# The lo part of the keys on both partition halves: score matmuls of 128 rows

## The chip, the cores and the metric

The kernel runs on one core of a Trainium2 chip. The core has a tensor engine (PE) for matmuls, VectorE (DVE), ScalarE (ACT) and GpSimd (POOL) for everything elementwise, and SyncE (SP), whose queue here issues the loads of weights. Each engine works through its own list of instructions in order and waits on semaphores for the others. The metric is device time in microseconds of one execution; lower is better.

## The reference

One decoder layer on 256 tokens of width 1024, in float32: a SwiGLU half-step, then a mixer stage, a memory cross-attention and a second SwiGLU half-step, each followed by a layer norm. The mixer stage runs a state-space branch (SSD) beside a sparse attention (DSA); the change is in DSA.

```
q_idx, k_idx, w_idx: index queries (16 heads of 64), one index key of 64, 16 head weights
score[q, s] = sum over h of relu(q_idx[q, h] . k_idx[s]) * w_idx[q, h] / 4, causal
keep the 64 best keys s of every query q
s[q, h, k]  = q[q, h] . (w_uk c_kv)[k, h] / 8 - slope[h] * (q - k), on the kept keys
o[q, h]     = softmax(s) (w_uv c_kv)
```

c_kv is a normalised latent of 256 per token, from which keys and values of the 16 heads of 64 are made.

## The kernel before

Every float32 operand a is split on the chip into hi (a rounded to the float32r format) and lo = a - hi; a product is hi.hi + hi.lo + lo.hi, three passes on PE that accumulate in PSUM (`mm3`). `split` (line 144) makes hi with a cast on ACT and lo with a subtraction on DVE. Weights are loaded in pieces of 128 x 1024 into four `raw` buffers and split into `whi` and `wlo`, six buffers each (`weight`, line 89). A block of work on PE (`a_block`) is 24 matmuls of 128 x 256.

**The scores.** Heads are 64 wide, half of the 128 partitions. `project` (line 633) therefore packs the queries: in one tile hi stands on one partition half and lo on the other. The first score matmul contracts over all 128 rows, the packed queries against keys whose hi stands on both halves (`kh`), and so gives hi.hi + lo.hi in one pass. The second takes the 64 rows of the queries' hi against the 64 rows of the keys' lo:

```
self.mm(o, q[:, hh // 2, ts], kh, True, False)
self.mm(o, q[r, hh // 2, ts], kl[r], False, True)
```

`scores` (line 646) does this for two blocks of 128 queries: four matmuls per head into one of two score banks (`ps_s`). It runs for 16 heads of the index (line 664, keys `kidxh` and `kidxl`), whose relu on ACT frees the bank and whose sum over the heads is made on DVE into `acc`, and for 16 heads of the attention (`softmax_in`, line 687, keys of the tile `kv`). `kidxl` is made from a transposed key that already stands on both halves, so all its 128 rows are filled.

**Keys and values.** `keys_values` (line 748) runs four times, for four heads each. It makes the keys in a PSUM bank and copies them out: per pair of heads two ACT copies (hi to both halves) and one DVE subtraction (lo to one half), then the values' hi and lo of token block 0 (`vh`, `vl`), all in one tile `kv` of 2048 columns: 1024 for hi, 512 for lo, 512 for the values.

**The order.** `fly` (line 117) interleaves three streams, DSA, SSD and a filler (keys and values, the gates, the SSD output projection), by an estimate of PE time: a stream yields how long it wants to wait for the other engines. After the index heads come 16 rounds of maximum and replacement on DVE (the top-k) while PE does filler work; then step by step (line 734) scores of one head, the transposes of the head two steps earlier and the values of the head three steps earlier, with 2.4 us (by the estimate) of filler between. The SSD stream ends with a product by silu(z) on DVE (line 608), a mean of squares on ACT, a power on POOL and a scaling on ACT (line 616); PE then transposes the result. On each engine the framework that builds the program settles the final sequence by its own schedule, so a change of one instruction can shift neighbours.

Of the kernel before, what the change touches and what calls it, by code (L numbers as in the profile page):

```python
"""Hybrid decoder layer (macaron SwiGLU, Mamba-2 SSD beside DSA attention, memory
cross-attention, SwiGLU; DeepNorm post-LayerNorms) on one core.

float32 products go through the tensor engine as three float32r passes: every
operand a is split on the chip into hi (a rounded to float32r) and lo = a - hi,
and a.b = hi.hi + hi.lo + lo.hi accumulates in PSUM.  Small products stay float32.
"""
# [12 lines left out]
F32 = mybir.dt.float32  # L20
F32R = mybir.dt.float32r
# [4 lines left out]
P = 128  # L26
T = 256
# [6 lines left out]
HD = 64  # L34
# [4 lines left out]
ALPHA = 2.0 ** 0.25  # L39
# [11 lines left out]
class Layer:  # L51
# [37 lines left out]
    def weight(self, ap, piece=1024, pool=False):  # L89
        """loads, split into (hi, lo) in pieces of columns; pool: GpSimd makes the last lo."""  # L90
        out = []
        for c in range(0, ap.shape[1], piece):
            raw = self.raw()[:, :piece]
            hi = self.wp.tile([P, 1024], F32R, tag="whi", name=self.nm("whi"), bufs=6)[:, :piece]
            lo = self.wp.tile([P, 1024], F32R, tag="wlo", name=self.nm("wlo"), bufs=6)[:, :piece]
            self.nc.sync.dma_start(raw, ap[:, c:c + piece])
            self.split(raw, hi, lo, self.nc.gpsimd if pool and c else self.nc.vector)
            out.append((hi, lo))
        return out
# [17 lines left out]
    def fly(self, *streams):  # L117
        """emits several streams of work in one order: a stream yields after a piece either
        how long (us of matmul work) its next piece should wait for the other engines, or the
        name of a result that another stream marks as done."""  # L120
        live = [[g, self.pe, None] for g in streams]
        while live:
            ok = [e for e in live if e[2] is None or e[2] in self.done]
            now = [e for e in ok if e[1] <= self.pe]
            e = now[0] if now else min(ok, key=lambda e: e[1])
            self.pe = max(self.pe, e[1])
            e[2] = None
            try:
                r = next(e[0])
            except StopIteration:  # L130
                live.remove(e)
                continue
            if isinstance(r, str):
                e[2] = r
            else:
                e[1] = self.pe + r

    def mm3(self, out, a, b, start, stop):
        """out (+)= a^T b; a, b = (hi, lo)."""
# [8 lines left out]
    def a_block(self, ps, w, xT):  # L148
        """w: (hi, lo) [p, 128] per K block, stationary; ps [128 features, 256 tokens]."""
# [3 lines left out]
    def a_unit(self, ap, xT):  # L153
        """two 128-column blocks, [p, (2, kb, 128)], by 256 tokens in one bank."""
# [11 lines left out]
    def b_part(self, ps, w, xT, tb, k, start, stop):  # L166
        """tokens of block tb stationary, one K block w (hi, lo) [p, n] moving."""
# [11 lines left out]
    def b_chunk(self, wap, xT, evac, width=512):  # L179
        """[2, p, (4 kb, width)] columns, both token blocks in turn."""  # L180
# [32 lines left out]
    def constants(self):  # L213
# [7 lines left out]
        # attention keys: [0:256] for the queries of block 1, [256:384] for block 0  # L221
# [27 lines left out]
    def ln_params(self, i):  # L249
        """(scale, shift) of layer norm i, each as two halves of the columns."""  # L250
        out = []
# [13 lines left out]
    def layer_norm(self, r, st, gb, dst):  # L265
        """r [128, 1024] with bn statistics st; dst may be r."""
# [11 lines left out]
    def res_evac(self, ps, c, r, x, scale, st):  # L278
        """r = scale * ps + x in the columns from c, with their statistics."""
# [11 lines left out]
    def ffn_in(self, win, xT, slots, first=None, by_token=0):  # L291
        """silu(gate) * up as hi/lo by features; the first by_token units run one token block
        after the other, so that the matmuls need not wait for the second."""
# [35 lines left out]
    def first_units(self, xT):  # L329
        """tokens and the first two units of FFN 1 K block by K block, as they arrive; the  # L330
        tensor engine and the activation tables are warmed up meanwhile."""
# [32 lines left out]
    def ffn_out(self, wout, act, finish, skew=3, last=False):  # L364
        """last: the columns that end last are finished in two parts."""
# [27 lines left out]
    def z_proj(self, xT):  # L393
        """silu(z), token-major; block 0 of the tokens runs ahead."""
# [12 lines left out]
    def xbc(self, xT, xtok, bc):  # L407
        """convolution and silu by features; x goes back to token-major."""
# [30 lines left out]
    def small_proj(self, xT):  # L439
        """c_kv, dt, w_idx and k_idx, token-major."""  # L440
# [17 lines left out]
    def latent(self, cT):  # L458
        """normalised c^T as hi/lo."""
# [18 lines left out]
    def k_index(self, kidx):  # L478
        """k_idx^T on both halves of the partitions."""
# [7 lines left out]
    def softplus(self, x, n):  # L487
        """log(1 + exp(x)) = max(x, 0) + 2 atanh(e / (2 + e)), e = exp(-|x|), x [128, n]."""
# [19 lines left out]
    def ssd_decay(self):  # L508
        """dt, the cumulated decays, and these as rows on every partition (DMA)."""
# [30 lines left out]
    def ssd(self, zs, xtok, bc, yT):  # L540
        """y takes the place of x in xtok."""
# [85 lines left out]
    def dsa(self, xT, kidx, cT, oT):  # L627
        """index scores, top-k, attention over the selected keys; o^T as hi/lo."""
# [4 lines left out]
        def project(name, u, scale):  # L633
            """(hi; lo) of the even heads and (lo; hi) of the odd ones on the partition halves."""
# [11 lines left out]
        def scores(q, hh, kh, kl):  # L646
            """kh: hi on both partition halves, kl: lo."""
            r, q = slice((hh % 2) * HD, (hh % 2 + 1) * HD), q[hh % 2]
            ps = self.psum("s")
            for tb in range(NTB):  # L650
                o, ts = ps[:, (1 - tb) * 256:(2 - tb) * 256], slice(tb * P, (tb + 1) * P)
                self.mm(o, q[:, hh // 2, ts], kh, True, False)
                self.mm(o, q[r, hh // 2, ts], kl[r], False, True)
# [25 lines left out]
        # attention  # L679
# [7 lines left out]
        def softmax_in(h):  # L687
            u, hh = h // 4, h % 4
            kv = self.kv[u]
            ps = scores(qs[u], hh, kv[0][:, hh % 2, hh // 2, :], kv[1][:, hh // 2, :])  # L690
# [11 lines left out]
        def turn(h):  # L702
            """p^T: key block 0 by all queries as hi/lo, key block 1 by the queries of block 1."""
# [10 lines left out]
        def values(h):  # L714
# [6 lines left out]
            # both heads of a pair are stationary, one of them is meant  # L721
# [26 lines left out]
    def keys_values(self, u, cT):  # L748
        """keys of four heads by features (hi of the even heads and of the odd ones on both
        partition halves, lo), their values by tokens (hi/lo of block 0; block 1)."""  # L750
# [4 lines left out]
        kl = s[:, 1024:1536].rearrange("p (a b) -> p a b", b=T)  # L755
        vh, vl = s[:, 1536:1792], s[:, 1792:]
# [5 lines left out]
        for i in range(2):  # L762
            a, b = slice(i * HD, (i + 1) * HD), slice((1 - i) * HD, (2 - i) * HD)
            nc.scalar.copy(kh[a, i], ps[a])
            nc.vector.tensor_sub(kl[a], ps[a], kh[a, i].bitcast(F32))
            nc.scalar.copy(kh[b, i], ps[a])
        yield 0.0
# [85 lines left out]
    def proj_ln(self, wap, inT, x, gb, done, hooks=()):  # L853
        """x <- LN(x + in W) in place, x pre-scaled by ALPHA; the last K blocks of the input
        come late, and token block 0 ends before block 1."""
# [33 lines left out]
    def run(self):  # L889
        nc, t = self.nc, self.t  # L890
# [96 lines left out]
def layout(x, mem, ffn1_w_in, ffn1_w_out, ln1_g, ln1_b, w_in, conv_w, conv_b, dt_bias, a_log, d_skip,  # L987
# [5 lines left out]
    def feats(w):                       # [1024, 256 n] -> [n, p, (2, kb, 128)]  # L993
# [3 lines left out]
    def toks(w, width=512):             # [1024, width n] -> [n, 2, p, (4 kb, width)]  # L997
# [3 lines left out]
    def ffn(win, wout, by_token=0):  # L1001
# [4 lines left out]
        if not by_token:                # the first two units by K block: [k, (gate, up) x 2, 128]  # L1006
# [43 lines left out]
```

## Time and profile before

| | us |
|---|---|
| median of 3 runs | 835.6 |
| lowest and highest | 834.26, 835.91 |
| span of the profiled execution | 833.3 |
| PE, DVE, ACT, POOL busy in it | 816.3, 560.8, 424.1, 68.1 |
| index heads on PE | about 297 to 347 |
| attention heads on PE | about 367 to 480 |

The span runs from the first to the last instruction of the profiled execution; its own time is the span and what lies around it, which the profile does not show. A row of a timeline has the start, the length and the instruction, out<-in with the program's names, and in brackets the idle time before it and what ended it. Matmuls are pipelined: one is listed with 0.28 us and the next starts after 0.12 us, so costs on PE are read from start to start, and PE's busy time is no measure of work done. The form 64*128 or 128*128 is the height and width of the stationary operand. A row of busy times has the length of the stretch, the busy time of each engine with its number of instructions, the clock that PE was granted (1.00 is 2.4 GHz, 0.50 is 1.2 GHz), and the share and rate of the DMA engines.

### The profile page before, as it was taken

Reading aid. Unit: us, or ns where it says so; the run is one execution under the profiler, and the core shown is the slowest. Engines: PE = TensorE matmul, PEld = TensorE weight load, DVE = VectorE, ACT = ScalarE, POOL = GpSimd, SP = SyncE. Lnnn points to the kernel's source line nnn. Section 1 sums busy time; section 2 is a strip of 40 time slices with the busy share of each in tenths; the row PEclk is TensorE's granted clock in tenths of the full one; section 3 lists DMA queues with packets and bytes.
Section 4 is the critical chain, followed back from the end, with each engine's and each line's share of the span. In section 5 each row is a group of like instructions: output and inputs, shape, how many; then the busy total and the mean of one; then the engine's idle time right before and its main releaser. Section 6 shows DMA issues by size and latency. Waiting matters only on the chain.

```text
span 833.3 us, 14320 instructions
## 1 busy us (share of the span) xinstructions
PE 816.3 (98%) x5726; PEld 758.1 (91%) x5726; DVE 560.8 (67%) x870; ACT 424.1 (51%) x700; POOL 68.1 (8%) x69
## 2 busy tenths in 40 slices
PE   8999999999989899999999999999999999999996
PEld 7999999887889887899999998889988999999885
DVE  5665555449598988598778767965659755555445
ACT  5564444324666584477566545454444644444430
POOL 1100000000024351130000000100001000000000
PEclk9999999999999998999999999999999999999998
DMA  7886555554556513226444355685434755555531
GB/s 246 275 281 212 178 181 184 194 176 130 193 191 240 180 49 107 72 77 217 150 126 153 117 174 182 199 271 172 151 119 134 260 184 179 187 190 179 185 120 51
DMA packets 39923, 142.97 MB, mean 172 GB/s; under 512 B 4592, under 2 KB 4896, under 8 KB 39472
## 3 DMA queue, kind: packets, MB, share of 16 engines
q1 hardware_dynamic: 38016, 134.63, 49.0%
q0 software_dynamic: 1840, 7.43, 2.9%
q8 instruction: 45, 0.74, 0.4%
q14 instruction: 22, 0.18, 0.1%
HBM read 140.97 MB, written 1.06 MB: 170 GB/s over the span
## 4 chain that ended last, share of the span: by engine, by line
PE 89%; DVE 4%; issue 4%; DMA 1%; ACT 1%; POOL 0%; SPq 0%; DVEq 0%; ACTq 0%; POOLq 0%
PE ps_mm L111 79%; PE ps_s L111 5%; DVE wlo L146 2%; PE ps_t L115 2%; PE ps_t L111 2%; DMA raw<-in_ffn_in_dram 1%; DVE wa L430 1%; ACT whi L145 0%; DVE spp L503 0%; DVE bcT L430 0%; POOL rstd L262 0%; DVE bst L285 0%; ACT L432 0%; SPq L349 0%; DVE x L282 0%
## 5 line engine op out<-in xcount | busy, mean ns | idle before, releaser
L146 DVE TENSOR_TENSOR wlo<-raw,whi 128x1024 fp32r<-128x1024 f32 (+2 forms) x245 | 302.2, 1236 | 184.8 <-ACT whi L145 183.3
L145 ACT CAST whi<-raw 128x1024 fp32r<-128x1024 f32 (+2 forms) x253 | 262.4, 1041 | 222.1 <-PE ps_mm L111 111.5
L111 PE MATMUL ps_mm<-x1Th,whi 128*128 128x256 f32 x384 | 112.4, 293 | 0.0
L111 PE MATMUL ps_mm<-x1Tl,whi 128*128 128x256 f32 x384 | 110.9, 289 | 0.0
L111 PE MATMUL ps_mm<-x1Th,wlo 128*128 128x256 f32 x384 | 110.8, 289 | 0.0
L111 PE MATMUL ps_mm<-x0Th,whi 128*128 128x256 f32 x352 | 99.7, 285 | 1.4 <-ACT whi L145 1.3
L111 PE MATMUL ps_mm<-x0Tl,whi 128*128 128x256 f32 x352 | 99.2, 283 | 0.0
L111 PE MATMUL ps_mm<-x0Th,wlo 128*128 128x256 f32 x352 | 98.3, 284 | 0.7 <-DVE wlo L146 0.7
L111 PE MATMUL ps_mm<-x3Th,whi 128*128 128x256 f32 x304 | 86.2, 284 | 0.0
L111 PE MATMUL ps_mm<-x3Th,wlo 128*128 128x256 f32 x304 | 86.0, 283 | 0.0
L111 PE MATMUL ps_mm<-x3Tl,whi 128*128 128x256 f32 x304 | 86.0, 283 | 0.0
L111 PEld LDWEIGHTS ps_mm<-x1Th,whi 128*128 128x128 f32 x384 | 75.5, 197 | 1.3
L111 PEld LDWEIGHTS ps_mm<-x1Tl,whi 128*128 128x128 f32 x384 | 75.5, 197 | 0.4 <-issue 0.4
L111 PEld LDWEIGHTS ps_mm<-x1Th,wlo 128*128 128x128 f32 x384 | 75.7, 197 | 0.1
L111 PEld LDWEIGHTS ps_mm<-x0Th,whi 128*128 128x128 f32 x352 | 67.7, 192 | 2.5 <-ACT whi L145 2.5
L111 PEld LDWEIGHTS ps_mm<-x0Th,wlo 128*128 128x128 f32 x352 | 66.9, 192 | 1.3 <-DVE wlo L146 1.3
L111 PEld LDWEIGHTS ps_mm<-x0Tl,whi 128*128 128x128 f32 x352 | 67.7, 192 | 0.0
L111 PE MATMUL ps_mm<-whi,ah 128*128 128x512 f32 x154 | 60.4, 392 | 0.0
L111 PE MATMUL ps_mm<-wlo,ah 128*128 128x512 f32 x154 | 60.1, 390 | 0.0
L111 PE MATMUL ps_mm<-whi,al 128*128 128x512 f32 x154 | 59.9, 389 | 0.0
L111 PEld LDWEIGHTS ps_mm<-x3Tl,whi 128*128 128x128 f32 x304 | 58.4, 192 | 0.0
L111 PEld LDWEIGHTS ps_mm<-x3Th,wlo 128*128 128x128 f32 x304 | 58.4, 192 | 0.0
(305 smaller groups left out, 1708.9 us busy)
## 6 DMA issues: line engine op xcount, KB each, us to landing
raw<-in_ffn_in_dram SPq DMA_DIRECT2D x87, 512.0 KB, 4.4
raw<-in_ffn_out_dram SPq DMA_DIRECT2D x44, 512.0 KB, 4.4
raw<-in_w_xbc_dram SPq DMA_DIRECT2D x16, 512.0 KB, 4.3
raw<-in_w_gate_dram SPq DMA_DIRECT2D x16, 512.0 KB, 3.6
raw<-in_w_z_dram SPq DMA_DIRECT2D x8, 512.0 KB, 4.4
raw<-in_w_qidx_dram SPq DMA_DIRECT2D x8, 512.0 KB, 4.1
raw<-in_w_q_dram SPq DMA_DIRECT2D x8, 512.0 KB, 3.7
raw<-in_w_pssd_dram SPq DMA_DIRECT2D x8, 512.0 KB, 4.1
```

The lines of the kernel that those rows point to most:

```text
L111: self.nc.tensor.matmul(out, a, b, start=start, stop=stop)
L115: self.nc.tensor.transpose(out, in_, self.ident)
L145: self.nc.scalar.copy(hi, src)
L146: (engine or self.nc.vector).tensor_sub(lo, src, hi.bitcast(F32))
L430: self.last_conv = nc.vector.scalar_tensor_tensor(v[:, d:], src[:, :T - d], cw[:, 3 - d:4 - d], v[:, d:], op0=ALU.mult, op1=ALU.add)
```

## The change

The lo of the keys now stands on both partition halves, as hi does. The second score matmul then takes the whole packed queries (128 rows) against it; it adds lo.lo to the product. For this `keys_values` makes two DVE subtractions per pair of heads instead of one, after both ACT copies, and `kl` takes 1024 columns of the tile `kv`. The values' hi and lo move to a buffer of the tag `w2c` (two buffers, also used by the SSD stream and the cross-attention). The index keys need nothing new. Comments and docstrings are gone from the file as well, with no effect on the program.

```
         def scores(q, hh, kh, kl):
-            r, q = slice((hh % 2) * HD, (hh % 2 + 1) * HD), q[hh % 2]
+            q = q[hh % 2]
...
                 self.mm(o, q[:, hh // 2, ts], kh, True, False)
-                self.mm(o, q[r, hh // 2, ts], kl[r], False, True)
+                self.mm(o, q[:, hh // 2, ts], kl, False, True)
...
-            ps = scores(qs[u], hh, kv[0][:, hh % 2, hh // 2, :], kv[1][:, hh // 2, :])
+            ps = scores(qs[u], hh, kv[0][:, hh % 2, hh // 2, :], kv[1][:, hh % 2, hh // 2, :])
...
-        kl = s[:, 1024:1536].rearrange("p (a b) -> p a b", b=T)
-        vh, vl = s[:, 1536:1792], s[:, 1792:]
+        kl = s[:, 1024:].rearrange("p (i a b) -> p i a b", i=2, b=T)
+        v0 = self.small([P, 2, T], "w2c", F32R, 2)
+        vh, vl = v0[:, 0, :], v0[:, 1, :]
...
             nc.scalar.copy(kh[a, i], ps[a])
-            nc.vector.tensor_sub(kl[a], ps[a], kh[a, i].bitcast(F32))
             nc.scalar.copy(kh[b, i], ps[a])
+            nc.vector.tensor_sub(kl[a, i], ps[a], kh[a, i].bitcast(F32))
+            nc.vector.tensor_sub(kl[b, i], ps[a], kh[a, i].bitcast(F32))
```

The sequence of PE keeps its matmuls, since the estimate counts columns and these are the same. What moves is seen on ACT and DVE. First ACT at the first unit of keys, in the midst of the index heads: `kv` are the copies of the keys and the cast of the values, `wa<-ps_s` the relus, `whi` casts of weights, `w2a` the scaling of the next index queries. Before:

```order
L666 ACTIVATE wa_3255<-ps_s_3250 128x384
L145 CAST whi_3661<-raw_3660 128x1024
L766 CAST kv_3204<-ps_mm_3206 64x512
L764 CAST kv_3204<-ps_mm_3206 64x512
L145 CAST whi_3774<-raw_3773 128x1024
L766 CAST kv_3204<-ps_mm_3206 64x512
L641 ACTIVATE w2a_3328<-ps_mm_3267 64x512
L666 ACTIVATE wa_3339<-ps_s_3334 128x384
L666 ACTIVATE wa_3352<-ps_s_3347 128x384
```

And now:

```order
L666 ACTIVATE wa_3258<-ps_s_3253 128x384
L145 CAST whi_3658<-raw_3657 128x1024
L145 CAST whi_3664<-raw_3663 128x1024
L765 CAST kv_3204<-ps_mm_3207 64x512
L766 CAST kv_3204<-ps_mm_3207 64x512
L145 CAST whi_3777<-raw_3776 128x1024
L641 ACTIVATE w2a_3331<-ps_mm_3270 64x512
L666 ACTIVATE wa_3342<-ps_s_3337 128x384
L666 ACTIVATE wa_3355<-ps_s_3350 128x384
```

Before, the second copy of the first pair of heads (766) stands here, then the two of the second pair (764, 766) with a weight cast between. Now the first pair's second copy stands ahead of this piece, right behind its first, and only the second pair's two copies (765, 766) are left, one behind the other. The cast, the scaling and the relus behind them keep their places.

Then DVE at the same place: `kv` are the subtractions of the keys (and, at 128 x 256, of the values), `acc` the sum over the index heads, `w2b` and `E` the SSD stream, `wlo` the lo of a weight. Before:

```order
L580 TENSOR_TENSOR E_2639<-E_2639,w2b_3182 128x1024
L765 TENSOR_TENSOR kv_3204<-ps_mm_3206,kv_3204 64x512
L669 SCALAR_TENSOR_TENSOR acc_3015<-wa_3230,widx_2227,acc_3015 128x256
L669 SCALAR_TENSOR_TENSOR acc_3015<-wa_3230,widx_2227,acc_3015 128x128
L146 TENSOR_TENSOR kv_3204<-ps_mm_3234,kv_3204 128x256
L669 SCALAR_TENSOR_TENSOR acc_3015<-wa_3255,widx_2227,acc_3015 128x256
L669 SCALAR_TENSOR_TENSOR acc_3015<-wa_3255,widx_2227,acc_3015 128x128
L765 TENSOR_TENSOR kv_3204<-ps_mm_3206,kv_3204 64x512
L571 TENSOR_TENSOR w2b_3264<-ps_t_3259,triu 128x512
L146 TENSOR_TENSOR wlo_3383<-raw_3381,whi_3382 128x1024
L580 TENSOR_TENSOR E_2643<-E_2643,w2b_3264 128x1024 x2
L642 SCALAR_TENSOR_TENSOR w2a_3328<-ps_mm_3267,w2a_3328 64x512
```

And now:

```order
L580 TENSOR_TENSOR E_2639<-E_2639,w2b_3182 128x1024
L767 TENSOR_TENSOR kv_3204<-ps_mm_3207,kv_3204 64x512
L768 TENSOR_TENSOR kv_3204<-ps_mm_3207,kv_3204 64x512
L669 SCALAR_TENSOR_TENSOR acc_3015<-wa_3233,widx_2227,acc_3015 128x256
L669 SCALAR_TENSOR_TENSOR acc_3015<-wa_3233,widx_2227,acc_3015 128x128
L146 TENSOR_TENSOR w2c_3205<-ps_mm_3237,w2c_3205 128x256
L669 SCALAR_TENSOR_TENSOR acc_3015<-wa_3258,widx_2227,acc_3015 128x256
L669 SCALAR_TENSOR_TENSOR acc_3015<-wa_3258,widx_2227,acc_3015 128x128
L767 TENSOR_TENSOR kv_3204<-ps_mm_3207,kv_3204 64x512
L768 TENSOR_TENSOR kv_3204<-ps_mm_3207,kv_3204 64x512
L571 TENSOR_TENSOR w2b_3267<-ps_t_3262,triu 128x512
L146 TENSOR_TENSOR wlo_3386<-raw_3384,whi_3385 128x1024
```

Each subtraction of the keys has a second one behind it, and the values' lo goes to `w2c`; all that follows stands two rows later.

## Rows read from the trace of the kernel before

**Rows 1.** The page, sections 1 and 4: engines, and shares of the chain.

```profile
PE 816.3 (98%) x5726; PEld 758.1 (91%) x5726; DVE 560.8 (67%) x870; ACT 424.1 (51%) x700; POOL 68.1 (8%) x69
...
PE 89%; DVE 4%; issue 4%; DMA 1%; ACT 1%; POOL 0%; SPq 0%; DVEq 0%; ACTq 0%; POOLq 0%
```

**Rows 2.** Busy time by stretch; then PEclk, DMA share, GB/s.

```profile
299.46:313.20 13.74, 13.74 (x99) 12.19 (x98) 13.52 (x18) 10.31 (x16) 6.19 (x4) 1.00 0.00 0
316.40:323.10 6.70, 6.70 (x24) 5.36 (x24) 4.44 (x9) 2.62 (x4) 1.34 (x1) 0.50 0.10 35
299.46:339.70 40.24, 40.24 (x240) 33.56 (x238) 34.69 (x48) 20.71 (x33) 11.15 (x6) 0.92 0.29 92
354.50:366.90 12.40, 12.40 (x106) 12.40 (x105) 12.31 (x58) 8.86 (x18) 3.40 (x2) 1.00 0.25 86
382.25:411.01 28.76, 28.76 (x218) 26.71 (x216) 22.25 (x44) 19.81 (x45) 0.64 (x1) 1.00 0.55 173
411.01:439.77 28.76, 28.76 (x218) 26.72 (x216) 22.55 (x46) 18.20 (x45) 0.54 (x1) 1.00 0.44 139
```

**Rows 3.** Timeline of PE (start, length), first attention head.

```profile
366.78 0.28 PE L111 MATMUL ps_mm<-x1Th,wlo 128*128 128x256 f32 x1
366.90 1.21 PE L111 MATMUL ps_s<-kv,w2a 128*128 128x256 f32 x4
368.04 0.39 PE L111 MATMUL ps_mm<-x1Th,whi 128*128 128x256 f32 x1
368.27 0.28 PE L111 MATMUL ps_mm<-x1Tl,whi 128*128 128x256 f32 x1
```

**Rows 4.** Timeline of PE, first scores of the cross-attention.

```profile
571.64 0.28 PE L111 MATMUL ps_s<-mkh,w2a 128*128 128x256 f32 x1
571.76 0.27 PE L111 MATMUL ps_s<-mkl,w2a 128*128 128x256 f32 x1
```

**Rows 5.** Instructions on the score banks: the full-height weight load.

```profile
L111 PEld LDWEIGHTS ps_s<-mkl,w2a x16: 187/188/190, 571.6 to 614.2; 128*128 128x128 f32 x16
```

**Rows 6.** Timeline of PE while the clock is at its lower level.

```profile
317.30 0.58 PE L111 MATMUL ps_s<-kidxh,w2e 128*128 128x256 f32 x1
317.81 0.58 PE L111 MATMUL ps_s<-kidxl,w2e 64*128 64x256 f32 x1
...
319.72 0.41 PE L111 MATMUL ps_mm<-x1Th,wlo 128*128 128x256 f32 x1
319.93 0.41 PE L111 MATMUL ps_mm<-x1Th,whi 128*128 128x256 f32 x1
```

**Rows 7.** Instructions on the kv tile: the subtraction (min/median/max ns).

```profile
L765 DVE TENSOR_TENSOR kv<-ps_mm,kv x8: 678/689/695, 309.4 to 449.4; 64x512 fp32r<-64x512 f32 x8
```

**Rows 8.** Timeline of ScalarE, first unit of keys.

```profile
310.12 0.58 ACT L766 CAST kv<-ps_mm 64x512 fp32r<-64x512 f32 x1 [1.95 <-DVE kv L765]
...
314.53 0.49 ACT L666 ACTIVATE wa<-ps_s 128x384 f32<-128x384 f32 x1 [0.52 <-PE ps_s L111]
```

**Rows 9.** Timeline of all engines: from silu(z) to the SSD transposes.

```profile
339.70 1.22 DVE L608 TENSOR_TENSOR xtok<-xtok,zs 128x1024 f32<-128x1024 f32 x1
...
341.03 0.42 ACT L612 ACTIVATE wa<-xtok 128x256 f32<-128x256 f32 x1 [5.17 <-DVE xtok L608]
...
347.02 1.42 POOL L262 TENSOR_TENSOR rstd<-rstd,mhalf 128x4 f32<-128x4 f32 x1 [10.32 <-DVE rstd L261]
...
348.47 1.71 ACT L616 ACTIVATE xtok<-xtok,rstd 128x256 f32<-128x256 f32 x4 [0.47 <-POOL rstd L262]
...
354.52 1.03 PE L115 MATMUL ps_t<-ident,xtok 128*128 128x128 f32 x8
```

**Rows 10.** Timeline of PE, the first head's transposes.

```profile
381.76 0.49 PE L115 MATMUL ps_t<-ident,wa 128*128 128x128 f32 x3
```

**Rows 11.** Timeline of PE after an idle time.

```profile
245.16 0.47 PE L115 MATMUL ps_t<-ident,wb 128*128 128x128 f32 x1 [2.89 <-DVE cTl L475]
...
245.65 0.41 PE L111 MATMUL ps_mm<-x1Th,whi 128*128 128x256 f32 x1
```

## The prediction

> **What bounds the kernel now.** I read the page's busy totals and its chain first: the tensor engine (PE) is busy 98% of the span, and 89% of the chain that ended last is PE [rows 1]. A total hides stages, so next the busy time by stretch [rows 2]. Where the changed matmuls lie, from 297 to 473 us, PE is busy for the whole of every stretch, and the view of waits has no wait of PE at all from 300 to 500 us. So PE sets the pace there, and each microsecond that leaves its stream counts, until some other engine cannot follow. VectorE (DVE) is the one to watch: 34.69 of 40.24 us in the index stage, 12.31 of 12.40 where the top-k begins, 78% (22.25 of 28.76) over four heads of attention [rows 2]. Third, the order of PE's instructions in time, for what a score matmul costs.
>
> **Part 1, the score matmuls.** A head is a group of four: hi, lo for one token block, hi, lo for the other. The hi ones contract over 128 rows, the lo ones over 64. Ordinary 128-row matmuls of this shape start 0.12 us apart (366.78 to 366.90). The group starts at 366.90, the matmul behind it at 368.04, and the next at 368.27: five starts take 1.37 us where five ordinary ones take 0.60 [rows 3]. The excess is 0.77 us, and it is paid at each change of height: the matmul behind the group still pays one (0.23 to the next start), though it is itself ordinary. Cross-attention has the control: its scores, hi and lo both over 128 rows, of the same shape, start 0.12 us apart [rows 4]. After the change the group has that form throughout, so I take the whole 0.77 us out. There are 16 groups of the index and 16 of the attention: 16 x 0.77 = 12.3 us each, 24.6 in all, on PE, which waits for nothing.
>
> A rule of the Trainium skill speaks against this ("TensorE: Matmul & The Clock Gate", Part 3, The mechanism): a weight load overlaps a running matmul only where the row groups differ. By it a full-height load behind a full-height matmul is exposed, and the change would give nothing. The trace disagrees: full-height loads of 188 ns run under matmuls that start 0.12 us apart [rows 4, 5].
>
> **Part 2, the clock.** In two places the granted clock falls from the upper level (2.4 GHz) to the lower (1.2 GHz): from 316.35 to 323.1 and from 347.1 to 350.5. In the first the granted clock reads 0.50 [rows 2]. Both times PE had just run score groups nearly back to back, in which a start came each 0.31 us. At the lower level score matmuls start 0.51 apart instead of 0.31, and ordinary ones 0.21 instead of 0.12 [rows 6]. Over both places that is 16 + 10 ordinary ones at 0.093, 2.4 us, and some nine starts of score matmuls at up to 0.20, 1.8 us: 4.2 us. When score groups run as densely as the rest, what went before the falls is gone; I let these 4.2 us go too. Ends: 0 (the falls come all the same) and 4.2.
>
> **Part 3, the evacuation of the keys.** Each of four units gets two more DVE subtractions of 64 x 512 from PSUM. The same form is there: 0.69 us each [rows 7], so 8 x 0.69 = 5.5 us of DVE, 1.4 per unit; reading one partition half and writing the other is what the split of the queries (line 642) does already, so I see no surcharge. ScalarE's two copies of a pair of heads now stand together, as the order shows: its wait of 1.95 us for the first subtraction [rows 8] moves to the first copy of the unit's second pair, which waits for the first pair's subtractions, now two: some 0.6 us later. Queued behind it are a weight cast, the scaling of the next queries and the relus that free the two score buffers. The values' move into a buffer of their own costs nothing: the same cast and subtraction write it, and no transfer is added; the weights come in the same sequence, but for one exchange of neighbours.
>
> **Part 4, what is late next: the index stage.** On PE alone, the transposes of the SSD output that stand at 354.52 [rows 9] would come 12.3 + 4.2 = 16.5 us earlier, at 338.0. Their input hangs on DVE: a product by silu(z) that starts at 339.70, then four squares on ScalarE, the power on GpSimd (1.42) and the scaling [rows 9]. DVE was idle 40.24 - 34.69 = 5.55 us between 299.46 and 339.70 [rows 2]; if it never idled, with 1.4 us of new subtractions, that product would start at 335.5. From there to the first scaled half (half of 1.71) it was 9.6 us, with relus that waited for PE between; the pure work is 1.22 + 4 x 0.42 + 1.42 + 0.86 = 5.2 us. So the input is there between 340.7 and 345.1. I take 8 us (the chain shares both queues with other work), 343.5. PE is then held 5.5 us, and the stage gives 16.5 - 5.5 = 11.0 us. An earlier hold lies inside this one: the third group of the second index unit needs a score buffer that a relu of ScalarE frees; that relu ran at 314.53 behind the key copies [rows 8], and PE would want the buffer near 311.
>
> The top-k comes next on DVE, but PE needs its result late, for the first head's transposes at 381.76 [rows 10], 15 us behind the stretch in which DVE does the top-k [rows 2]. This gap absorbs the rest of DVE's lag.
>
> **Part 5, the attention.** 16 groups give 12.3 us. Over four heads PE would need 28.76 - 4 x 0.77 = 25.7 us, DVE 22.25 + 1.38 = 23.6 (then 22.55 + 1.38 = 23.9): 92 to 93% [rows 2]. What PE loses to that, no stretch of the attention shows. Lower end 0: with DVE at 99% (354.50 to 366.90) and at 98% (299.46 to 313.20) PE lost nothing [rows 2], because weights are split several blocks ahead. Upper end 7 us, a share as in the index stage (5.5 of 12.3 and more). I take 1.5, since 92% is below both stretches without loss.
>
> **Part 6, idle and clock.** Before 245.16 PE idled 2.89 us for DVE, and the matmul at 245.65 took 0.41 us instead of 0.28, as at the lower level [rows 6, 11]. A hold in the index stage can do that again: some 16 matmuls at 0.093 are 1.5 us; I take half, 0.8.
>
> **Sum.** 11.0 + 12.3 - 1.5 - 0.8 = 21.0 us. The profiled execution spans 833.3 us; the three timed runs have 834.26 to 835.91, so 1.0 to 2.6 us lie around the span, and nothing there changes. The span becomes 812.3; against the median, 835.6 - 21.0 = 814.6 us.
>
> **The rivals.**
> A. PE alone counts. Holds vanish because the order has slack I don't see: 12.3 + 12.3 + 4.2 = 28.8, 806.8 us. For it: no wait of PE from 300 to 500 now. Against: the product at 339.70 would have to move by more than DVE's idle time allows.
> B. DVE and ScalarE hold PE in the attention too. The hold of 7 us there, and the index stage at its lower end (345.1, so 9.4): 9.4 + 12.3 - 7 - 0.8 = 13.9, 821.7 us. For it: 92% leaves DVE 1.8 us in 25.7, and it works in order, so a subtraction that waits for its cast stops the softmax steps behind it. Against: the two stretches at 98 and 99%.
> C. The change of height is not what costs; a lo matmul stays at 0.31. Its price in rows: a load of 0.188 and a stream of 0.12 laid end to end are 0.31, just what a score matmul takes now. Then nothing is gained, the subtractions hide in DVE's idle time: 835.6 to 836.6. Against: [rows 4]. This is what the rule of the Trainium skill in part 1 would come to.
> D. Slower. The holds of the index stage throw the clock to the lower level for most of it. Each matmul there costs 0.093 us more; it takes 21.0 / 0.093 = 225 of them to eat the gain, and the 240 between 299.46 and 339.70 [rows 2] make 22.3: 835.6 - 21.0 + 22.3 = 836.9 us. For it: the fall after an idle of 2.89 us. Against: a PE that waits for DVE anyway loses less by a slow clock.
>
> **Chances.** The forecast 0.61 (811 to 819 by itself), A 0.13, B 0.19, C 0.04 (0.03 of it within 0.2%), D 0.03. About 0.2% is what a measurement of this kernel can tell from no change. Faster: 0.61 + 0.13 + 0.19 = 0.93; same 0.03; slower 0.04. The range takes in A and most of B: 806.5 to 823.5 us.
>
> **What would show it.** Score matmuls and the first one behind a group at 0.12 us between starts, all of 128 rows; if the second is so and the first not, part 1 fails. No lower clock at the score groups (part 2). In the index stage PE waits appear, for ScalarE's relus or scalings or DVE's query splits, 4 to 8 us in all, and the transposes of the SSD output about 11 us earlier (part 4). In the attention 4.3 us from head to head where 5.0 was, DVE above 90%, PE waits of 0 to 3 us (part 5). The forecast is wrong if PE waits over 6 us in the attention, or if the index stage ends over 14 us or under 8 us earlier.

## Result and profile after

The changed kernel takes 821.5 us (median of 4 runs, 820.32 to 824.07) beside 835.75 (4 runs, 834.26 to 837.31): a ratio of 0.9839, interval 0.9815 to 0.9863. The profiled execution spans 820.1 us, 13.2 less than before (14.2 by the medians); forecast were 21.0. First the page's totals and its chain, which answer to [rows 1]:

```profile
PE 796.0 (97%) x5726; PEld 753.3 (92%) x5726; DVE 561.5 (68%) x878; ACT 422.2 (51%) x700; POOL 68.3 (8%) x69
...
PE 73%; DVE 9%; issue 9%; DMA 4%; ACT 3%; POOL 1%; SPq 0%; DVEq 0%; POOLq 0%; ACTq 0%
```

PE lost 20.3 us of busy time. But the span lost 13.2: the chain runs over PE for 73% in place of 89%. The score matmuls themselves became what part 1 said. The timeline of PE at the second attention head:

```profile
366.65 0.28 PE L111 MATMUL ps_mm<-x1Th,wlo 128*128 128x256 f32 x1
366.77 0.64 PE L111 MATMUL ps_s<-kv,w2e 128*128 128x256 f32 x4
367.24 0.28 PE L111 MATMUL ps_mm<-x1Th,whi 128*128 128x256 f32 x1
367.36 0.28 PE L111 MATMUL ps_mm<-x1Tl,whi 128*128 128x256 f32 x1
```

From the group's start to the second start behind it: 0.59 us, where [rows 3] have 1.37. So the 0.77 per group went, the matmul behind it included. Read in the same way, each of the 14 groups behind the first head's transposes takes 0.67 or 0.68 us, and took 1.45 or 1.46 before. Where the rest stayed is seen in PE's waits from 300 to 500 us (in total, times, longest); before there was none. In the names, `wa` is a relu of the index at line 666 and the probabilities of a head at line 700; `w2a` and `w2e` are packed queries, `S0xe` the SSD state, `yTl` the lo of the transposed SSD output, `w2d` and `wc` parts of the transposed probabilities:

```profile
PE ps_s L111 <- ACT wa L666: 2.6, 1, 2.6
PE ps_s L111 <- DVE w2a L642: 1.2, 1, 1.2
PE ps_mm L111 <- ACT S0xe L587: 1.1, 1, 1.1
PE ps_mm L111 <- DVE w2d L146: 0.9, 3, 0.5
PE ps_t L115 <- DVE yTl L204: 0.8, 1, 0.8
PE ps_t L115 <- DVE wa L700: 0.4, 1, 0.4
PE ps_mm L111 <- ACT wc L711: 0.3, 1, 0.3
```

The first of them is the hold that part 4 named. On ScalarE the copy of the second pair of heads waits for the doubled subtractions (1.95 us in [rows 8], 3.40 now), and the relus stand behind it:

```profile
312.01 0.58 ACT L765 CAST kv<-ps_mm 64x512 fp32r<-64x512 f32 x1 [3.40 <-DVE kv L768]
312.61 0.58 ACT L766 CAST kv<-ps_mm 64x512 fp32r<-64x512 f32 x1
313.09 1.04 ACT L145 CAST whi<-raw 128x1024 fp32r<-128x1024 f32 x1
314.16 0.59 ACT L641 ACTIVATE w2a<-ps_mm 64x512 fp32r<-64x512 f32 x1
314.65 0.85 ACT L666 ACTIVATE wa<-ps_s 128x384 f32<-128x384 f32 x2
```

PE starts the group that needs that bank at 315.18, and comes out of the wait at the lower clock: ordinary matmuls 0.21 apart until 318.3, as in [rows 6].

```profile
312.32 0.28 PE L111 MATMUL ps_mm<-x1Th,whi 128*128 128x256 f32 x1
315.18 0.58 PE L111 MATMUL ps_s<-kidxh,w2a 128*128 128x256 f32 x1 [2.58 <-ACT wa L666]
...
317.05 0.41 PE L111 MATMUL ps_mm<-x1Tl,whi 128*128 128x256 f32 x1
317.26 0.41 PE L111 MATMUL ps_mm<-x1Th,wlo 128*128 128x256 f32 x1
...
318.50 0.28 PE L111 MATMUL ps_mm<-x1Th,wlo 128*128 128x256 f32 x1
318.62 0.28 PE L111 MATMUL ps_mm<-x1Th,whi 128*128 128x256 f32 x1
```

The first row shows that a wait costs more than the idle that is listed: the matmul ahead of it runs its 0.28 us to the end, where an ordinary one is followed after 0.12. From start to start that is 2.86 us, 0.16 more than the idle of 2.58 and the ordinary 0.12.

A second such fall lies behind the wait of 1.1 us at 329.95, over the products of SSD. Busy time by stretch, the clock behind POOL's column: first index group to the middle of the index, to the SSD transposes, to the first attention scores, to the first head's transposes, and two times four heads:

```profile
298.65:323.30 24.65, 22.07 (x175) 21.87 (x174) 22.31 (x28) 15.92 (x26) 10.10 (x6) 0.93 0.07 22
323.30:348.06 24.76, 23.65 (x162) 22.77 (x161) 20.20 (x37) 11.99 (x28) 4.84 (x3) 0.86 0.25 86
348.06:361.84 13.78, 12.54 (x107) 12.37 (x105) 13.72 (x57) 9.32 (x23) 4.37 (x3) 1.00 0.45 153
361.84:376.32 14.48, 13.63 (x113) 13.43 (x114) 13.35 (x35) 9.58 (x27) 2.38 (x1) 1.00 0.30 96
376.32:403.34 27.02, 26.29 (x219) 25.82 (x218) 24.37 (x47) 20.14 (x45) 0.64 (x1) 1.00 0.59 198
403.34:429.60 26.26, 26.03 (x219) 25.83 (x218) 23.57 (x48) 18.23 (x44) 0.54 (x1) 1.00 0.51 165
```

DVE is at 90% over four heads (24.37 of 27.02) where [rows 2] have 77% (22.25 of 28.76). Two marks in PE's timeline, for [rows 9, 10]: the SSD transposes came 6.5 us earlier (354.52 before), the first head's 5.4 (381.76).

```profile
348.06 0.38 PE L115 MATMUL ps_t<-ident,xtok 128*128 128x128 f32 x2
...
376.32 0.27 PE L115 MATMUL ps_t<-ident,wa 128*128 128x128 f32 x1
```

**Where the gain went.** I call "the approach" the stretch from the first index group to the first head's transposes. Its length can be taken apart in every kernel: PE's idle time, what the lower clock cost (an estimate: half of PE's busy time at that level, read in stretches of 2 us; by the starts of ordinary matmuls, 0.21 us apart in place of 0.12, it would be 43%), and the rest, PE's own work at the upper level. Beside it DVE's busy time in the approach, the attention from the first head's transposes to the last, and the ratio to before with its interval (us; worked out from the windows and timelines of one profiled execution each):

```
kernel           approach  idle  clock  own work   DVE  attention  ratio
before               84.3   0.0    5.1      79.2  69.3       94.4  1
changed              77.7   5.8    4.9      67.0  69.6       86.6  0.9839 [0.9815, 0.9863]
e1 index             81.4   6.6    6.5      68.3  72.4       94.4  0.9969 [0.9949, 0.9990]
e2 attention         83.2   0.0    5.1      78.0  69.2       86.4  0.9902 [0.9865, 0.9938]
e3 evacuation        83.0   0.0    3.4      79.6  69.3       94.4  0.9997 [0.9979, 1.0016]
e4 casts first       78.6   6.6    4.6      67.5  69.4       86.7  0.9866 [0.9837, 0.9895]
e5 filler            91.8  11.4   11.1      69.3  72.3       85.2  0.9976 [0.9954, 0.9997]
e6 scalar first      76.9   6.9    2.8      67.2  67.7       90.0  0.9871 [0.9839, 0.9903]
e7 pool, index       80.8   8.9    4.8      67.1  72.9       85.2  0.9859 [0.9829, 0.9888]
e8 pool, attention   83.3   9.3    7.5      66.6  73.5       89.2  0.9935 [0.9913, 0.9956]
e9 order             83.1   9.4    7.0      66.8  69.1       86.9  0.9836 [0.9817, 0.9855]
e10 queries first    81.0   8.3    6.2      66.5  70.1       85.7  0.9880 [0.9860, 0.9899]
e11 no division      77.6   5.9    4.8      66.8  68.5       84.6  0.9800 [0.9780, 0.9820]
e12 halves by DMA    84.0   8.6    8.8      66.6  72.3       87.3  0.9915 [0.9898, 0.9933]
```

The change took 12.2 us from PE's own work in the approach (79.2 to 67.0). 5.8 of it went into idle, and the clock cost as much as before. What is left is 6.6, with 7.8 from the attention. DVE, with 69.6 us, now has more to do there than PE. The profiled execution of e9 is 5.3 us slower than its median, so one row can be some us off. DVE's column counts a blocked instruction as busy: each row of 72 us or more (e1, e5, e7, e8, e12) has in its approach at least one subtraction of a weight's lo that took 2.7 us or more beside one of GpSimd, where 1.22 is usual (see e8).

### The profile page after: what moved, and what is told of

Its sections match the earlier page's. It is cut to its first block, busy times and chain, and to the rows that moved or that the text cites. A ratio compares the mean times of both kernels' runs of the same rounds, so it can differ in the third digit from the quotient of the medians.

```text
span 820.1 us, 14322 instructions
## 1 busy us (share of the span) xinstructions
PE 796.0 (97%) x5726; PEld 753.3 (92%) x5726; DVE 561.5 (68%) x878; ACT 422.2 (51%) x700; POOL 68.3 (8%) x69
## 4 chain that ended last, share of the span: by engine, by line
PE 73%; DVE 9%; issue 9%; DMA 4%; ACT 3%; POOL 1%; SPq 0%; DVEq 0%; POOLq 0%; ACTq 0%
PE ps_mm L111 68%; DVE wlo L146 2%; PE ps_t L111 2%; PE ps_t L115 2%; DMA raw<-in_ffn_in_dram 1%; PE ps_s L111 1%; ACT whi L145 1%; DVE acc L669 1%; POOL wlo L146 1%; DVE acc L676 1%; DVE m L675 1%; DMA raw<-in_w_qidx_dram 0%; DMA cs_rows<-wa 0%; DMA raw<-in_w_pssd_dram 0%; POOL rstd L262 0%
## 5 line engine op out<-in xcount | busy, mean ns | idle before, releaser
L146 DVE TENSOR_TENSOR wlo<-raw,whi 128x1024 fp32r<-128x1024 f32 (+2 forms) x245 | 299.7, 1226 | 182.1 <-ACT whi L145 180.2
```

Of the source, the lines that this page charges most:

```text
L146: (engine or self.nc.vector).tensor_sub(lo, src, hi.bitcast(F32))
```

## The experiments

**The change in parts.** The emission order comes from a scheduler that uses its own estimates; e2 and e3 have exactly the order of the changed kernel on PE, DVE and ScalarE, e1 exactly that of before. So these three compare cleanly.

```
-                self.mm(o, q[:, hh // 2, ts], kl, False, True)
+                if whole:
+                    self.mm(o, q[:, hh // 2, ts], kl, False, True)
+                else:
+                    self.mm(o, q[r, hh // 2, ts], kl[r], False, True)
```

> Only the 16 index groups contract over 128 rows; the attention's scores and the keys' evacuation are those of the kernel before. Theory 1 (in the index stage some 4.5 of the 12.3 us that the groups free are lost again, to relus and copies that PE waits for and to the lower clock, and the new subtractions have little to do with it): saves 7 to 9, so 827 to 829 us, SSD transposes 6 to 8 us earlier than before. Theory 2 (the loss of the index stage comes from ScalarE's copy of the second pair, which stands behind the doubled subtractions, absent here): saves 10 to 11.5, 824 to 826 us.

Measured: 832.3 us, 0.31% faster, far less than either theory. The SSD transposes came 7.5 us nearer to the first index group, as theory 1 had it; but then PE waited for DVE, still in the top-k and its followers, and the clock fell again. The two longest of its waits from 285 to 500 us:

```profile
PE ps_s L112 <- ACT wa L670: 4.0, 2, 2.7
PE ps_t L116 <- DVE yTl L205: 2.4, 1, 2.4
```

Theory 2 fell in its simple form: PE waits for relus (4.0 us) without any doubled subtraction. The wait for `yTl` has a cause that no score matmul brings: ahead of it a subtraction of a weight's lo took DVE 3.21 us beside one of GpSimd.

```profile
361.84 2.41 POOL L147 TENSOR_TENSOR wlo<-raw,whi 128x1024 fp32r<-128x1024 f32 x1 [7.84 <-ACT whi L146]
362.12 3.21 DVE L147 TENSOR_TENSOR wlo<-raw,whi 128x1024 fp32r<-128x1024 f32 x1
```

In the changed kernel the two come one behind the other, and the wait is 0.8 us. So e1 shows too little by an estimated 2 us (3.21 - 1.22), which is most of what e1 and e2 (2.8 and 8.3 us by the medians) lack to the 14.2 of the whole change.

> Only the 16 attention groups contract over 128 rows, with the doubled lo of the keys; the index's lo matmuls stay at 64 rows. Theory 1 (the attention loses about 3 of its 12.3 us to waits for the values' operands, whatever the index stage does): saves 8 to 10, so 826 to 828 us. Rival (the attention's loss is a lag carried over from the index stage, which is as slow as before here): saves 11 to 12.3, 823.5 to 825 us.

Measured: 826.8 us, 0.98% faster. The attention is 86.4 us long, as in the changed kernel (86.6), with an approach as slow as before. So the attention's loss is its own and no lag carried over; the rival is out.

> The doubled subtractions and the values' buffer of the changed kernel, all score matmuls as before (lo over 64 rows). Theory 1 (DVE's idle time hides 8 x 0.69 us while PE is the slower one): 835 to 836.5 us, no wait of PE from 300 to 500 us. Rival (ScalarE's copies behind the doubled subtractions hold the relus and so PE even here): 838 us or more, with a PE wait for a relu near 315.

Measured: 835.35 us, no difference, and no wait of PE from 285 to 500 us. The new order and the doubled subtractions cost nothing while PE has 79.6 us of work of its own. The windows row of its approach: PE busy throughout, DVE 69.30.

```profile
300.46:383.45 82.99, 82.99 (x550) 72.99 (x549) 69.30 (x154) 48.01 (x102) 21.73 (x11) 0.96 0.22 75
```

**The holds of the index stage.** In e4 `keys_values` makes all four copies before the four subtractions; e6 has that and, in `project`, both scalings on ScalarE before both subtractions.

```
             nc.scalar.copy(kh[a, i], ps[a])
             nc.scalar.copy(kh[b, i], ps[a])
+        for i in range(2):
+            a, b = slice(i * HD, (i + 1) * HD), slice((1 - i) * HD, (2 - i) * HD)
             nc.vector.tensor_sub(kl[a, i], ps[a], kh[a, i].bitcast(F32))
```

> The changed kernel with the four hi copies of the keys ahead of the four subtractions, so that ScalarE's third copy no longer waits 3.4 us for DVE. Theory 2 (that wait, with the relus queued behind it, makes PE's idle of 2.6 us at 315 and the fall of the clock behind it): PE does not wait there, 817.5 to 820 us. Theory 1 (the hold only moves to another relu or to DVE, and the clock falls elsewhere): 820.5 to 822.5 us.

Measured: 824.4 us; no faster than the changed kernel. The wait at 315 is gone, but the next one is longer. PE's two longest waits in the approach:

```profile
PE ps_mm L111 <- ACT S0xe L587: 3.9, 1, 3.9
PE ps_s L111 <- DVE w2a L642: 1.3, 1, 1.3
```

And ScalarE's timeline at the first of them:

```profile
329.17 0.59 ACT L641 ACTIVATE w2e<-ps_mm 64x512 fp32r<-64x512 f32 x1 [3.73 <-DVE w2a L642]
329.78 0.58 ACT L587 COPY S0xe<-ps_mm 128x512 f32<-128x512 f32 x1
```

The hold moved, as theory 1 said, and again stands behind ScalarE waiting for DVE in queue order, now at the queries: that speaks for theory 2, and e6 takes this wait away too.

> The casts-first kernel, and in the index and attention queries too both scalings of ScalarE stand ahead of the two subtractions of DVE: ScalarE no longer waits for DVE in either (3.7 us for one such wait in the run before). Theory 2 (what holds PE in the index stage is ScalarE standing behind DVE, in queue order): the PE waits for relus and for the copy of the SSD state go, the SSD transposes come 3 us or more earlier than in the changed kernel, 816.5 to 819 us. Theory 1 (DVE's own work bounds the stage, ScalarE's waits only pass it on): waits for DVE take their place, 820.5 to 824 us.

Measured: 824.2 us: by the time, theory 1 (0.2 above its range). By the stage, theory 2: from the first index group to the SSD transposes 42.2 us (341.28 - 299.12) in place of 49.4, and up to the first attention scores the clock never falls. The windows rows from the first index group to these scores, and of the whole approach:

```profile
299.12:353.12 54.00, 48.43 (x395) 47.27 (x393) 50.22 (x117) 34.91 (x72) 18.50 (x9) 1.00 0.17 60
299.12:376.00 76.88, 69.96 (x551) 68.24 (x550) 67.65 (x154) 47.85 (x102) 21.95 (x10) 0.96 0.26 84
```

Then PE stands: the scheduler put the first scores earlier, and their queries' lo lies behind the top-k on DVE. The timeline of PE there:

```profile
353.12 0.93 PE L111 MATMUL ps_s<-kv,w2a 128*128 128x256 f32 x4 [4.58 <-DVE w2a L644]
354.33 1.19 PE L111 MATMUL ps_s<-kv,w2e 128*128 128x256 f32 x4 [0.28 <-DVE w2e L644]
356.60 0.58 PE L111 MATMUL ps_mm<-x1Th,wlo 128*128 128x256 f32 x1 [1.07 <-DVE wlo L146]
```

What the index stage gained, the top-k took back, and the attention became 3.4 us longer in the new order, half of it by the lower clock behind a wait of 2.2 us.

**The clock.** e5 puts 20 matmuls ahead of the group at 315.18:

```
+                if h == 6:
+                    idle = self.psum("t")[:, :T]
+                    for _ in range(20):
+                        nc.tensor.matmul(idle, xT[0][:, 0, 0:P], xT[0][:, 0, :], start=True, stop=True)
```

> The changed kernel with 20 matmuls that nobody reads (2.4 us at 0.12) just ahead of the group at 315.18, where PE idles 2.58 us for a relu. Theory 3 (the clock falls because PE idled: a hold is paid a second time at the lower clock): no lower clock right behind that group, the index stage 1 to 2 us shorter, 819.5 to 821 us. Rival (the fall comes anyway, as before the change, where no idle stood ahead of it, or the time is only lost at the next wait for DVE): the SSD transposes stay where they are within 0.5 us, 821 to 823 us.

Measured: 833.3 us. Neither theory: the scheduler moved some rows on ScalarE and DVE, PE then waited 7.6 us for S0xe and 3.5 for yTl, and the lower clock cost 11.1 us in place of 4.9. There was no lower clock right behind that group, which fits theory 3, but as a test of its price the run is void. It shows the price of long idles: the kernel that idles most pays most for the clock.

**DVE's amount of work.** e7 and e8 let GpSimd make some lo of the weights.

```
-            yield from self.a_steps(ps, t[name][u], xT)
+            yield from self.a_steps(ps, t[name][u], xT, name == "w_qidx")
```

> The changed kernel with the lo of the last weight piece of each index query unit made by GpSimd in place of DVE: four pieces, some 4.9 us of DVE's work in the index stage. Theory 1 (DVE's work bounds the index stage): holds of PE shrink by 2 to 4 us before the transposes of the first head, 817.5 to 819.5 us. Theory 2 or the clock as the main cause: within 1 us of the changed kernel, 820.5 to 822.5 us; a slow GpSimd piece that PE waits for would show as a PE wait for wlo.

Measured: 823.8 us, above either range, and an approach 3.1 us longer in the profile: theory 1's gain did not come. DVE was busy 72.9 us there in place of 69.6, though it had less to do: two of its subtractions of a lo took 2.80 and 2.82 us beside GpSimd's. The attention, which the edit leaves alone, became 1.4 us shorter than in the changed kernel.

> The changed kernel with the lo of the last piece of each weight that lies in the attention (queries, SSD output projection, second gate) made by GpSimd: some 11 pieces of 1.22 us off DVE, which was 90% busy there. Theory 1 (the attention loses some 3 us of its 12.3 to DVE, which comes late with the operands of the values): from the first head's transposes to the last 85 us or less in place of 86.6, 819 to 820.5 us. Rival (the loss is the order in which a head's steps are put, not DVE's amount of work): 86.6 us as now, 821 to 822.5 us.

Measured: 829.5 us, slower than the changed kernel; neither. DVE's weight subtractions in the attention, grouped (count, busy us, mean ns, idle before them):

```profile
L146 DVE TENSOR_TENSOR wlo<-raw,whi 128x1024 fp32r<-128x1024 f32 x13 | 20.0, 1540 | 8.3 <-ACT whi L145 8.3
```

The changed kernel has 1218 ns there, over 24 of them. And one of these beside GpSimd, in the timeline:

```profile
394.42 2.40 POOL L146 TENSOR_TENSOR wlo<-raw,whi 128x1024 fp32r<-128x1024 f32 x1 [4.55 <-ACT whi L145]
394.87 3.04 DVE L146 TENSOR_TENSOR wlo<-raw,whi 128x1024 fp32r<-128x1024 f32 x1
```

The subtraction takes 3.04 us and ends 1.09 us after GpSimd's; the mean rose to 1.54. The Trainium skill says this ("SBUF — State Buffer", SBUF: two separate sides): a DVE operation with two SBUF inputs and a GpSimd operation that reads SBUF lock each other out, and the row agrees. The blocked subtractions before the attention go the same way: 3.21 us in e1, 3.17 in e5, 2.80 and 2.82 in e7, 3.19 in e12, each ending 1.08 us after GpSimd's. So work given to GpSimd comes back to DVE as waiting.

> The changed kernel with the softmax's division left out (two DVE multiplications per head, 0.54 us; the probabilities stay unnormalised). Theory 1 for the attention (DVE at 90% comes late with the operands of the values): from the first head's transposes to the last 84 to 85 us in place of 86.6, PE's waits for w2d gone, 819 to 820.5 us. Rival (PE's loss there is the latency from transposes through ScalarE and DVE to the values, whatever DVE has to do besides): 86.3 us or more, 821 to 822.5 us.

Measured: 818.4 us, below either range. Without the division (8.8 us of DVE over 14 heads, by the rows of line 700; 0.63 a head, not the 0.54 expected) the attention takes 84.6 us by the table's mark, 2.0 less, as theory 1 had it. But the mark moved: the last head's transposes, in the changed kernel

```profile
462.88 0.49 PE L115 MATMUL ps_t<-ident,wa 128*128 128x128 f32 x3
```

and here, where the third stands behind other matmuls:

```profile
458.13 0.38 PE L115 MATMUL ps_t<-ident,wa 128*128 128x128 f32 x2
...
459.07 0.27 PE L115 MATMUL ps_t<-ident,wa 128*128 128x128 f32 x1
```

From the first head's transposes to the first score of the cross-attention the gain is 1.0 us (181.0 in place of 182.1). Another 2.7 us of the profiled execution lie ahead of the first index group (at 295.94 here, 298.65 in the changed kernel), which the edit does not touch. And e5 and e7, with the division in place, have an attention of 85.2 us, in which PE idles 0.8 us (1.5 in the changed kernel, 0.5 here). So DVE's amount of work can be worth about 1 us, but what comes before the attention moves it as much; that the amount is what PE loses to there is not shown. The division also stands between a head's scores and its transposes, a path that this run shortens as well.

**The order before the attention.**

```
+        qs = []
+        yield from project("w_q", 0, 0.125)
         for i in range(TOPK // 8):
```

> The changed kernel with three moves in the order of the stage before the attention: both scalings of an index query unit on ScalarE ahead of DVE's two subtractions; the four hi copies of the first key unit ahead of its subtractions; and the projection of the first attention queries put ahead of the top-k, so that their subtractions no longer stand behind it in DVE's queue. Theory 2 (what the change lost before the first head's transposes is queue order: ScalarE behind DVE, then the queries behind the top-k, 4.6 us of idle and some 3 us at the lower clock in the scalar-first run): first index group to SSD transposes 42 to 43 us (49.4 in the changed kernel), to the first head's transposes 67 to 70 us (77.7), so 811 to 815 us. Theory 1 (DVE's amount of work bounds the stretch): 74 us or more to the first head's transposes, 818 us or more.

Measured: 821.2 us, equal to the changed kernel. First index group to SSD transposes 47.1 us; then PE waited 8.4 us for the lo of a weight behind the top-k. Theory 2's sum did not come: with the queries out of the way, the next thing that PE needs from DVE stands there. Theory 1's bounds (74 us and 818 us or more) are met, but such a wait in queue order would meet them too.

```profile
361.22 0.58 PE L111 MATMUL ps_mm<-x1Th,wlo 128*128 128x256 f32 x1 [8.40 <-DVE wlo L146]
```

> Only the last of these moves: the projection of the first attention queries ahead of the top-k, everything else as in the changed kernel. Theory 2: the wait of 1.2 us for w2a at the first head goes and nothing else, 820 to 821.5 us. Rival (that wait is what carries DVE's lag into the attention, so more than itself comes back): 818 to 819.5 us.

Measured: 824.6 us, slower than either theory. The wait for `w2a` went, the one for `yTl` grew from 0.8 to 3.2 us. Counted from the first index group the top-k ended 2.1 us later: one of the queries' two subtractions now stands ahead of it, the other in its midst, where DVE also waits 0.56 us for ScalarE. The wait for S0xe grew too (1.1 to 2.5), ahead of anything that was moved; that is open.

```
-            nc.scalar.copy(kh[b, i], ps[a])
+            nc.gpsimd.dma_start(kh[b, i], kh[a, i])
...
-            nc.vector.tensor_sub(kl[b, i], ps[a], kh[a, i].bitcast(F32))
+            nc.gpsimd.dma_start(kl[b, i], kl[a, i])
```

> The changed kernel with the second partition half of the keys, hi and lo, filled by DMAs from the first (issued by GpSimd, 16 transfers of 64 x 512), in place of a second cast and a second subtraction: 8 x 0.69 us less on DVE and 8 x 0.58 less on ScalarE. Theory 1 (the amount of DVE's work is what both stretches give back; leaving 7.6 us of it out gave 2.0 us in the attention): about 1 us in the attention and 0.5 to 1.4 us before it, 819 to 820.5 us, and PE idles less than 5.8 us up to the first head's transposes. Rival (how DVE's queue falls out decides before the attention, not 1.4 us of work in it: idle has been 5.8 to 11.4 us there in eight orders): 821 to 825 us, with the attention 1 us shorter all the same.

Measured: 827.7 us, above either range. The rival held before the attention (84.0 us). In the attention the gain did not come either: PE waits for the transfers. Its waits from 290 to 480 us:

```profile
PE ps_s L111 <- ACT wa L666: 5.3, 2, 3.9
PE ps_t L115 <- DVE yTl L204: 3.2, 1, 3.2
PE ps_s L111 <- DMA kv<-kv: 2.6, 3, 1.2
```

No kernel that computes everything beats the changed one; e9 equals it.

## Why the prediction was right and wrong

The direction, the gain per group and the range held; the size did not: 13.2 us of span in place of 21.0 (by the medians 14.2, 821.5 where 814.6 was forecast). The missing 7.8 us by step:

- **Part 1** (the change of height) was right. The trace contradicts the rule weighed there, and rival C. That rule is one sentence of its section of the Trainium skill ("TensorE: Matmul & The Clock Gate", Part 3, The mechanism); another sentence there, which part 1 left out, also lets a load of the background weight buffer go ahead of running matmuls, so the section read whole does not speak against the change. In PE's own work it gave 12.2 us in the approach, where 18 groups at 0.77 make 13.8: 1.6 short. The 0.16 us that each of the four waits costs beyond its idle are 0.6 of that; the rest is open.
- **Part 2** (the falls of the clock go with the dense groups) fits where PE is hardly held: in e6 the clock stays at the upper level through the whole index stage; in e2 and e3, with the index at two heights, the falls come at about the places of before.
- **Part 6** is the term that was mis-sized. It set 0.8 us for the lower clock behind a hold; it cost 4.9, as much as before (5.1). Together parts 2 and 6 forecast a gain of 3.4 and 0.2 came: 3.2 short. In the changed kernel both falls follow an idle, of 2.58 and 1.11 us; that the idle brought them is likely and not shown, since a wait of 2.57 us at the same place in e10 had no fall behind it.
- **Part 4** had the sum of the holds before the attention nearly right (5.5 forecast, 5.8 measured) and the relu at 315 exactly, but not their places. They lie along the whole approach; only 7.7 us of the 11.0 had come at the SSD transposes, counted from the first index group (6.5 in all), under the 8 that was named as the limit. That PE waits there for the scaled SSD output, as [rows 9] suggested, was wrong: PE itself came late, and the transposes waited for nothing. Their input can come sooner than part 4 allowed: 43.2 us behind the first index group at the earliest by its sum (340.7 - 297.46), and by 42.2 in e6. The sentence that the top-k's gap absorbs DVE's lag failed: in the changed kernel itself the 1.2 us at 361.84 are for the queries' lo, which DVE makes at 361.00, right behind the top-k, and e6 and e9 show PE waiting there longer when it arrives earlier.
- **Part 3** cost nothing by itself (e3).
- **Part 5**: 14 heads gave 7.8 us of 10.8, so a loss of 3.0 where 1.5 was set: 1.5 short. e2 shows that it belongs to the attention and is no lag of the index stage; DVE's amount of work is shown for no more than about 1 us of it (e11). PE's five visible waits there are 1.6 us, and with 0.16 more for each 2.4 of the 3.0.
- 1.2 us lie ahead of the first index group, where nothing was changed. A fall of the clock at 281 us cost 1.7 us there; e3, e4, e6 and e9 have one at that place too, and before, e1, e2, e5, e8 and e10 to e12 don't.

1.6 + 3.2 + 0.3 + 1.5 + 1.2 = 7.8. Rival B's price (821.7) is what came, but not its mechanism: its 7 us of hold in the attention were 3.0, and it counted the same 3.4 us from the clock as the forecast. Of rival D, holds behind which the clock falls, 4.9 us came in place of 22.3, and the kernel before lost as much (5.1) without a hold. Rival A is what e6 nearly reached for the index stage: 14.9 us against its 16.5.

Open: whether DVE's amount of work or its order sets the approach, and the attention. No run took work off DVE without adding GpSimd's in its place or moving the order.

## What to carry to other kernels

Once the pacing engine has less work than the next one (67.0 against 69.6 us here), a hold taken away can return at the next instruction that stands behind the same queue, as in e4, e6 and e9: count the work of both engines over the whole stretch up to where the result is needed, not up to the first wait. Price a hold of PE at its length, 0.16 us more, and the time at the lower clock that can follow it; in the changed kernel's approach idle and clock cost about the same (5.8 and 4.9). In an order made by a scheduler, compare the order of every queue before reading an experiment: from e4 to e12 every run moved more than its edit, e10 least, and a mark of a stretch can move with it (e11).

## What was not expected of the hardware

- DVE's subtraction from SBUF stretches when one of GpSimd already runs: 1.22 us alone, 2.80 to 3.21 in the pairs named above, and its end lies 1.08 to 1.09 us behind the end of GpSimd's each time. Four of these pairs come from edits that were not about it (e1, e5, e12, the later one of e7): a shift in time is enough to bring such a pair together.
- The clock after an idle is not certain: behind waits of 2.5 to 2.9 us at about 280 us it fell in the changed kernel, e3, e4, e6 and e9 and stayed up in e1, e2, e5 and e10 to e12; the longest of these waits, 2.91 us in e5, had no fall.
- Moving half a tile from one partition half to the other by DMA took 2.2 to 6.5 us from issue to landing (median 4.6), where the subtraction takes 0.69 us on DVE.
